# Four modulation vectors in two pairs on three engines, and weight folds moved by one chunk, in a diffusion block's mixer

## The chip, the cores and the metric

One core of one Trainium2 chip. The metric is the device time of one execution in microseconds (us), smaller is better. Times below are the median of several executions, and one profiled execution, whose trace is read here. TensorE multiplies matrices, VectorE and ScalarE and GpSimd work on tiles in SBUF (the on-chip memory, 128 partitions), SyncE only issues DMAs. Each engine works through its own queue of instructions in order; a DMA that is issued from ScalarE's queue stands in that queue too.

## The reference, cut to what matters

```python
sh1, sc1, g1, sh2, sc2, g2 = split(silu(c) @ w_ada + b_ada, 6)      # each 2048 long
h = rms_norm(x, norm1_g) * (1 + sc1) + sh1                           # 512 latent, 256 context rows
q, k, v, g, z_f, z_b, u = split(h @ w_in)                            # 2048 x 4128
o = bidirectional chunked gated linear attention(q, k, v, gates(z_f, z_b))
y = concat(norm(o) * gla_norm_g * silu(g), real part of a 2-D DFT of u)
x = x + g1 * (y @ w_out)
h2 = rms_norm(x, norm2_g) * (1 + sc2) + sh2
x = x + g2 * expert_choice_moe(h2)                                   # 16 experts, top 64 rows each
return rms_norm(x, final_norm_g)
```

Everything is float32. The first two vectors of the modulation (sh1, sc1) come early, in another form. The four "modulation vectors" of this document are numbers 2 to 5: g1, sh2, sc2 and g2. Each is a product of a 2048-long vector with a 2048 x 2048 matrix of 16.8 MB, read once.

## The kernel before, in words

Pages: `PG` holds 24 buffers of 128 x 2048 float32 (1 MB each), handed out first in, first out. A page that is given back may be taken at once; the new user's first instruction then waits until the last instruction of the old one is done. `PG.get()` with no page free makes the planner run a waiting background step early (`bg.force`).

Stages in order: the modulation's first part with the k columns (to about 150 us), the small z columns, the v columns (two groups c = 0, 1 of eight weight chunks each, six row tiles per chunk: four latent, two context), the q columns (eight chunks), the g columns (two groups of eight), the u columns (sixteen folded chunks), the output projection (four column groups c of eight chunks, the last four of each folded), the router, and the experts in eight pairs. Matmuls are done in three passes on a rounded high part and a low part.

Weights of the projections come through `Stream` (lines 166 to 215). A chunk (512 KB) is loaded by `load` from ScalarE's queue into one half of `rawp`. `split` takes a page, ScalarE copies the chunk into its first half rounded (line 203), VectorE writes the rest into its second half (line 204). `take(j)` splits up to chunk j + 1 before chunk j is used, `done(j)` gives the page back after TensorE's last matmul on it. Folded chunks (u columns, last four of each projection group) first go through `fold`: VectorE adds the halves (line 189), GpSimd subtracts them (line 190).

Background work is put between the matmuls by `Background`: after each row tile the foreground calls `bg.tick(us)`, in planner units (1.3 per tile in the v and q columns), and every generator that is due runs to its next `yield delay`. This fixes the order of instructions in each queue; the time at which they run is the chip's.

`ada_rest(i, delay)` (line 458) makes modulation vector i. It takes one page as accumulator; then for each of 16 steps it loads one page of `w_ada2` from the sync queue and adds page x scalar to the accumulator on VectorE (line 470 for the first, 472 for the others), and gives the page back. It keeps up to two pages loaded (`depth=2`): the one for this step and, if a page is free at that moment, the next one:

```python
for k in range(NK):
    while nl < min(k + depth, NK) and (nl == k or PG.free):
        ring[nl] = PG.get()
        sync.dma_start(ring[nl], a["w_ada2"][i - 2, nl])
        nl += 1
```

After the steps come four column sums on TensorE (line 478), a copy, transposes by matmul (line 483) and small additions. Before the change, `rest1` runs vectors 2, 4 and 3 one behind the other from the start of the v columns at 3.4 units per step; `rest2` drains it in the output projection, computes `logit_row`, and runs vector 5 at 4.6 units.

What holds pages in the v columns: HL (rounded latent rows, 8), HC (rounded context rows, 4, given back after v), rawp, W2, KT, KCM, VC (one each), V (one, then two), two rounded chunks, and the modulation's accumulator and ring.

In the projection, when a column group ends, four blocks of X (the residual state) are updated on VectorE (lines 1022 to 1026), and `logits` transposes them for the router. `pump` loads the experts' pages into whatever is free once `rest2` is done, from the third group on.

Of the kernel before, what the change touches and what calls it, by code (L numbers as in the profile page):

```python
# [17 lines left out]
AF = mybir.ActivationFunctionType  # L18
OP = mybir.AluOpType
# [11 lines left out]
C_F8, C_SCAN, C_MF, C_MB, C_FOLD, C_F, C_S8, C_ALL = 342, 350, 1118, 1246, 1374, 1470, 3297, 3881  # L31
F_CT, F_ST, F_ROW, F_CC, F_SC, F_K64, F_ALL = 0, 514, 1026, 1283, 1411, 1539, 1827
FW0 = 48
RD = (3.4, 4.6)
AD = (4.0, 2.5)
FD = (2.5, 1.8)
LD = (3.0, 7.0)
YD = (2.0, 3.0, 3.0, 5.0, 2.0, 1.0, 2.0, 2.0, 2.0)


# [62 lines left out]
def body(tc, nc, a, out, sb, pp):  # L103
    sync, act, dve, pe, pool = nc.sync, nc.scalar, nc.vector, nc.tensor, nc.gpsimd
    bg = Background()
# [5 lines left out]
    def tmp():  # L111
        tpi[0] = (tpi[0] + 1) % 4
        return TP[:, tpi[0], :]
# [14 lines left out]
    scol = sb.tile([128, NK], F32, name="scol")  # L128
# [17 lines left out]
    def v3(p, k):  # L146
        return p.rearrange("p (k n) -> p k n", k=k)


    X = [PG.get() for _ in range(4)]  # L150
# [15 lines left out]
    class Stream:  # L166
# [10 lines left out]

        def load(self, q=act):
            if self.nl < len(self.chunks) and self.nl < (max(self.ns, self.nf) if self.ns in self.folded else self.ns) + 2:
                q.dma_start(self.raw(self.nl), self.chunks[self.nl])  # L180
                self.nl += 1

        def fold(self, j):
# [9 lines left out]
        def split(self):  # L193
            n = self.ns
            self.load()
            self.fold(n)
            if self.ahead and n + 1 in self.folded:
                self.load()
                self.fold(n + 1)
                self.load()  # L200
            src = self.fw[n % 2] if n in self.folded else self.raw(n)
            p = PG.get()
            act.activation(p[:, :1024].bitcast(F32R), src, AF.Copy)  # L203
            dve.tensor_sub(p[:, 1024:].bitcast(F32R), src, p[:, :1024])  # L204
            self.parts[n] = p
            self.ns += 1

        def take(self, j):
            while self.ns < min(j + self.hd, len(self.chunks)):
                self.split()  # L210
            w = self.parts[j].rearrange("p (s k n) -> p s k n", s=2, k=2).bitcast(F32R)
            return w[:, 0], w[:, 1]

        def done(self, j):
# [3 lines left out]
    ws = Stream([a["w_in"][i] for i in range(W0)] + [a["w_out"][i] for i in range(32)],  # L218
                set(range(FW0, W0)) | {W0 + 8 * c + j for c in range(4) for j in range(4, 8)})
# [235 lines left out]
    bg.add(gate_rows(), 3.0)  # L455


    def ada_rest(i, delay, depth=2):

        acc = PG.get()  # L460
        ring = {}
        nl = 0
# [3 lines that stand above are left out]
                sync.dma_start(ring[nl], a["w_ada2"][i - 2, nl])  # L466
                nl += 1
            p = ring.pop(k)
            if k == 0:
                dve.tensor_scalar(acc, p, scol[:, 0:1], None, op0=OP.mult)  # L470
            else:
                dve.scalar_tensor_tensor(acc, p, scol[:, k:k + 1], acc, op0=OP.mult, op1=OP.add)  # L472
            PG.put(p)
            yield delay
        yield AD[0]
        b = BK.get()
        for j in range(4):
            pe.matmul(b[32 * j:32 * j + 32, :], ones[:, :32], acc[:, j * 512:(j + 1) * 512], start=True, stop=True)
        t = acc[:, :512]
        act.copy(t, b)  # L480
        yield AD[1]
        for q in range(4):
            pe.matmul(b[:, 4 * q:4 * q + 4], t[:, q * 128:(q + 1) * 128], sel4, start=True, stop=True)
        o, bias = {2: (gc[:, 0, :], bg1), 3: (b2, bsh2), 4: (a2, bsc2), 5: (gc[:, 1, :], bg2)}[i]

        def qj(x):
            return x.rearrange("p (j q) -> p q j", q=4)
        dve.tensor_add(qj(o), b[:, :NK].rearrange("p (q j) -> p q j", q=4), qj(bias))
        if i == 4:
            dve.scalar_tensor_tensor(a2, a2, 1.0, n2c, op0=OP.add, op1=OP.mult)  # L490
        BK.put(b)
        PG.put(acc)
# [11 lines left out]
            yield 1.3  # L504

    def rest(*vectors):
        for i, delay in vectors:
            yield from ada_rest(i, delay)

    rest1 = rest((2, RD[0]), (4, RD[0]), (3, RD[0]))  # L510
    bg.add(rest1)


    def tokens(j0, tiles, evac, last=False):
# [38 lines left out]
    for j in range(8):  # L553
        whi, wlo = ws.take(24 + j)
        for n in range(NH):
            for kk in range(2):
                k = 2 * j + kk
# [293 lines left out]
        BK.put(b)  # L851

    def rest_out():
        bg.drain(rest1)
        yield from logit_row()
        yield from rest((5, RD[1]))

    rest2 = rest_out()

# [50 lines left out]

    bg.drain(hfold)
    ws.ahead = True
    bs = [BK.get() for _ in range(4)]
    for k in range(NK):
        whi, wlo = ws.take(FW0 + k)
        for t, f in enumerate(lat):
            h = (f(k, 0), f(k, 1))
            i = t // 2
# [17 lines left out]
    X = [PG.get() for _ in range(4)]  # L936
# [39 lines left out]
    def logits(c, t):  # L976

        b = BK.get()
        for j in range(4):
            pe.transpose(b[:, j * 128:(j + 1) * 128], X[t][:, (4 * c + j) * 128:(4 * c + j + 1) * 128], ident)  # L980
        if not XT:
            XT.append(PG.get())
            lgb.append(BK.get())
        xtv = v3(XT[0], 4)
        act.copy(xtv[:, :, t * 128:(t + 1) * 128], v3(b, 4))
        BK.put(b)
        yield LD[1]
        for j in range(4):
            pe.matmul(lgb[0][32 * j:32 * j + 32, t * 128:(t + 1) * 128], awr[:, 4 * c + j, :],
                      xtv[:, j, t * 128:(t + 1) * 128], start=c == 0 and t == 0, stop=c == 3 and t == 3, skip_group_check=True)  # L990

    for c in range(4):
        bs = [BK.get() for _ in range(4)]
        cs = slice(c * 512, c * 512 + 512)
        order = [(j, t) for j in range(8) for t in range(4)]
        if c == 3:
            order = order[:16] + [(j, t) for t in (0, 2, 1, 3) for j in range(4, 8)]
        for n, (j, t) in enumerate(order):
            if (j, t) == (4, 0):
                bg.drain(gen)  # L1000
            whi, wlo = ws.take(W0 + 8 * c + j)
            i, ts = t // 2, slice(t * 128, (t + 1) * 128)
            for k, q in ((2 * j, 0), (2 * j + 1, 1)) if j < 4 else ((4 + j, i),):
                h = [yt(k, s)[:, ts] for s in range(2)]
                pe.matmul(bs[t], h[0], whi[:, q, :], start=k == 0, stop=False, skip_group_check=True)  # L1005
                pe.matmul(bs[t], h[0], wlo[:, q, :], start=False, stop=False, skip_group_check=True)  # L1006
                pe.matmul(bs[t], h[1], whi[:, q, :], start=False, stop=k == 11 and t == 3, skip_group_check=True)  # L1007
            if t == 2 and j >= 4:

                for s, w in ((0, whi), (0, wlo), (1, whi)):  # L1010
                    pe.matmul(bs[2][0:1, :], dT[:, j - 4, s:s + 1], w[:, 0, :], start=False, stop=False,
                              skip_group_check=True)
            if t < 3 and j == 7:

                y = Y64[0][0:72, ts if t < 2 else slice(256, 257)].bitcast(F32R)
                pe.matmul(bs[t][0:128 if t < 2 else 1, :], y, W64[0][0:72, cs].bitcast(F32R), start=False, stop=True,
                          skip_group_check=True)
            bg.tick(1.3 if j < 4 else 0.75)
            if j == 7 and t >= 2:
                t0 = t - 2  # L1020
                ps, qs = tmp(), tmp()
                dve.tensor_mul(ps, bs[t0], g1[0][:, cs])
                dve.tensor_mul(qs, bs[t], g1[0][:, cs])
                for x, f in ((X[t0][:, cs], dve.tensor_sub), (X[t][:, cs], dve.tensor_add)):
                    dve.tensor_add(x, x, ps)
                    f(x, x, qs)
                for r in (t0, t):
                    act.activation(ps if r == t0 else qs, X[r][:, cs], AF.Square, accum_out=ssx[:, r, c:c + 1])
                    bg.add(logits(c, r), LD[0])
            if t == 3:  # L1030
                ws.done(W0 + 8 * c + j)
            if c == 3 and (j, t) == (3, 3):
                PG.put(*YG[0], *YG[1])
            if (c, j, t) == (2, 7, 3):
                bg.drain(rest2)
            if c >= 2 and t == 3 and not bg.has(rest2):
                ws.hd = 4
                pump(keep=max(0, min(ws.hd - len(ws.parts), len(ws.chunks) - ws.ns)))
        BK.put(*bs)
# [161 lines left out]
    for pr in range(8):  # L1201
        gu = [BK.get() for _ in range(4)]
        for kg in range(8):
# [9 lines left out]
            ps = [wp.pop(wi + i) for i in range(4)]  # L1213
            wi += 4
            for m in range(2):
                if pr == 0 and m and kg < 7:
                    gather(0, 2 * kg + 2, 2)
                for k2 in range(2):
                    k = 2 * kg + k2
# [45 lines left out]
        for c in range(4):  # L1265
# [7 lines left out]
            for f in range(2):  # L1273
                if f and c and not last:
                    combine(pr, c - 1)
                ps = [wp.pop(wi + i) for i in range(2)]
# [33 lines left out]
    for c in range(4):  # L1310
        acc = v3(ACC[c], 4)
        cs = slice(c * 512, c * 512 + 512)
        for t in range(4):
            if c >= 2:
                dve.scalar_tensor_tensor(acc[:, t, :], acc[:, t, :], rsf[:, t:t + 1], FG[0][:, cs], op0=OP.mult,
                                         op1=OP.mult)
# [113 lines left out]
```

## Time and profile before

| | us |
|---|---|
| median of 3 runs | 1890.49 (1885.64 to 1891.79) |
| profiled execution | 1892.82 |
| its span | 1891.0 |
| TensorE busy | 1702.4 (90%) |
| VectorE busy | 761.1 (40%) |
| ScalarE busy | 343.3 (18%) |
| GpSimd busy | 82.9 (4%) |

A trace's times count from the span's start. PE is TensorE's matmuls, PEld its weight loads, DVE VectorE, ACT ScalarE, POOL GpSimd, SP SyncE; a name with q behind it is that engine's queue. `L472` is line 472 of the kernel. In groups, "idle before" is the time for which an engine stood just before such an instruction, with what ended it. `pg<-in_w_ada` is a load into a page from the modulation weights.

### The profile page before, as it was taken

The page shows a single profiled execution, that of the slowest core. Times are in us where ns is not written, and L with a number is a line of the kernel's source. Part 1 is how long each engine was busy: PE and PEld are TensorE (multiplying, and loading weights), DVE is VectorE, ACT ScalarE, POOL GpSimd, SP SyncE. Part 2 cuts the span into 40 slices and gives each one's busy share as a digit, 9 for nine tenths or more (in the row PEclk, how much of TensorE's full clock was granted, in tenths as well). Part 3 has the DMA queues.
Part 4 walks back from the last instruction along what each step waited for, and adds up shares of the span by engine and source line. Part 5 has one row for each costly group of instructions (what it writes and reads, how often), then busy time and mean ns, then how long its engine had stood idle before and what let it go on. Part 6 is the DMA issues. An engine that isn't in the chain of part 4 may idle for free.

```text
span 1891.0 us, 21143 instructions
## 1 busy us (share of the span) xinstructions
PE 1702.4 (90%) x8756; PEld 1011.0 (53%) x8756; DVE 761.1 (40%) x1188; ACT 343.3 (18%) x593; POOL 82.9 (4%) x61
## 2 busy tenths in 40 slices
PE   5999999897677798888999999999999999999885
PEld 4777887686455586665455444444444444444322
DVE  5335677837656647654323113131120311303005
ACT  4222111335443412222000000000000000000013
POOL 0000000001222101111000000000000000000000
PEclk9999999998888899998999999999999999999998
DMA  9955788621124336626796999999999999999996
GB/s 380 382 216 205 296 307 316 243 67 56 34 69 157 133 134 218 237 96 280 320 363 252 391 419 419 420 419 420 420 419 420 420 419 420 420 419 417 407 420 260
DMA packets 89760, 572.36 MB, mean 303 GB/s; under 512 B 9872, under 2 KB 12344, under 8 KB 27176
## 3 DMA queue, kind: packets, MB, share of 16 engines
q1 hardware_dynamic: 75720, 521.44, 68.3%
q10 hardware_dynamic: 13944, 49.56, 7.6%
q8 instruction: 69, 1.13, 0.2%
q14 instruction: 27, 0.22, 0.0%
HBM read 566.77 MB, written 4.19 MB: 302 GB/s over the span
## 4 chain that ended last, share of the span: by engine, by line
PE 38%; DMA 18%; DVE 6%; ACT 2%; issue 1%; POOL 0%; ACTq 0%; DVEq 0%; SPq 0%; POOLq 0%
PE bank L1222 16%; DMA pg<-in_w_e_up 10%; PE bank L1281 9%; PE bank L1141 5%; DMA pg<-in_w_e_down 4%; PE bank L1184 2%; DMA pg<-in_w_e_gate 2%; DMA pg<-in_w_out 2%; DVE pg L204 1%; ACT pg L203 1%; PE bank L1006 1%; PE bank L1007 1%; PE bank L1005 1%; DVE pg L472 1%; PE bank L501 0%
## 5 line engine op out<-in xcount | busy, mean ns | idle before, releaser
L1222 PE MATMUL bank<-pg,pg 128*64 128x512 f32 x1856 | 435.2, 597 | 25.8 <-DMA pg<-in_w_e_up 14.2
L1222 PEld LDWEIGHTS bank<-pg,pg 128*64 128x64 f32 x1856 | 139.2, 136 | 287.8 <-issue 218.1
L1281 PE MATMUL bank<-pg,tp 128*64 128x512 f32 (+1 forms) x1056 | 233.3, 584 | 11.7 <-ACT tp L1249 10.8
L204 DVE TENSOR_TENSOR pg<-pg,pg 128x1024 fp32r<-128x1024 f32 x96 | 122.5, 1280 | 109.5 <-ACT pg L203 95.2
L1145 DVE TENSOR_SCALAR pg<-bank,a,b 128x128 f32<-128x128 f32 x116 | 41.4, 405 | 302.6 <-PE bank L1141 302.6
L1281 PEld LDWEIGHTS bank<-pg,tp 128*64 128x64 f32 x1056 | 74.5, 137 | 145.8 <-issue 124.1
L472 DVE SCALAR_TENSOR_TENSOR pg<-pg,scol,pg 128x2048 f32<-128x2048 f32 x60 | 140.9, 2349 | 27.1 <-DMA pg<-in_w_ada 26.6
L203 ACT ACTIVATE pg<-pg 128x1024 fp32r<-128x1024 f32 x96 | 100.9, 1058 | 268.7 <-DVE pg L472 79.3
L523 PE MATMUL bank<-pg,pg 128*128 128x512 f32 x320 | 131.8, 412 | 13.6 <-ACT pg L203 13.6
L1187 DVE TENSOR_TENSOR pg<-pg,bank 128x512 f32<-128x512 f32 (+1 forms) x132 | 79.6, 666 | 152.9 <-PE bank L1184 152.9
L524 PE MATMUL bank<-pg,pg 128*128 128x512 f32 x320 | 128.8, 402 | 2.2 <-DVE pg L204 2.2
L525 PE MATMUL bank<-pg,pg 128*128 128x512 f32 x320 | 128.1, 400 | 0.0
L1141 PEld LDWEIGHTS bank<-pg,pg 128*128 128x128 f32 x896 | 104.0, 192 | 32.1 <-issue 29.2
L1141 PE MATMUL bank<-pg,pg 128*128 128x128 f32 x896 | 111.5, 279 | 0.0
L1256 ACT ACTIVATE tp<-bank 128x512 f32<-128x512 f32 x16 | 9.4, 597 | 431.4 <-PE bank L1222 431.4
L1005 PE MATMUL bank<-pg,pg 128*128 128x512 f32 x192 | 80.3, 418 | 5.5 <-ACT pg L203 5.5
L1006 PE MATMUL bank<-pg,pg 128*128 128x512 f32 x192 | 78.5, 409 | 5.7 <-DVE pg L204 5.7
L523 PEld LDWEIGHTS bank<-pg,pg 128*128 128x128 f32 x320 | 62.3, 195 | 30.4 <-ACT pg L203 14.9
L1007 PE MATMUL bank<-pg,pg 128*128 128x512 f32 x192 | 77.1, 402 | 0.0
L1285 DVE SCALAR_TENSOR_TENSOR pg<-bank,gcol,pg 128x512 f32<-128x512 f32 (+1 forms) x33 | 24.2, 735 | 125.1 <-PE bank L1281 125.0
L360 PE MATMUL bank<-pg,pg 128*128 128x512 f32 x192 | 71.8, 374 | 0.9 <-ACT pg L350 0.8
L524 PEld LDWEIGHTS bank<-pg,pg 128*128 128x128 f32 x320 | 62.4, 195 | 15.8 <-DVE pg L204 3.3
(318 smaller groups left out, 1974.2 us busy)
## 6 DMA issues: line engine op xcount, KB each, us to landing
pg<-in_w_e_gate SPq DMA_DIRECT2D x128, 1024.0 KB, 19.9
pg<-in_w_e_up SPq DMA_DIRECT2D x128, 1024.0 KB, 8.0
pg<-in_w_e_down SPq DMA_DIRECT2D x126, 1024.0 KB, 19.9
pg<-in_w_ada SPq DMA_DIRECT2D x96, 1024.0 KB, 7.6
pg<-in_w_in ACTq DMA_DIRECT2D x62, 512.0 KB, 4.4
pg<-in_w_out ACTq DMA_DIRECT2D x32, 512.0 KB, 3.4
pg<-in_x SPq DMA_DIRECT2D x4, 1024.0 KB
pg<-in_x_slots SPq DMA_DIRECT2D x4, 1024.0 KB, 12.4
```

The costliest lines, as they stand in the source:

```text
L203: act.activation(p[:, :1024].bitcast(F32R), src, AF.Copy)
L204: dve.tensor_sub(p[:, 1024:].bitcast(F32R), src, p[:, :1024])
L472: dve.scalar_tensor_tensor(acc, p, scol[:, k:k + 1], acc, op0=OP.mult, op1=OP.add)
L523: pe.matmul(bs[t], h[0], whi[:, kk, :], start=k == 0, stop=False)
L524: pe.matmul(bs[t], h[0], wlo[:, kk, :], start=False, stop=False)
L525: pe.matmul(bs[t], h[1], whi[:, kk, :], start=False, stop=k == 15)
L1005: pe.matmul(bs[t], h[0], whi[:, q, :], start=k == 0, stop=False, skip_group_check=True)
L1006: pe.matmul(bs[t], h[0], wlo[:, q, :], start=False, stop=False, skip_group_check=True)
L1007: pe.matmul(bs[t], h[1], whi[:, q, :], start=False, stop=k == 11 and t == 3, skip_group_check=True)
L1141: pe.matmul(b[:, j * 128:(j + 1) * 128], X[t][:, k * 128:(k + 1) * 128], ohr[:, t, :], start=t == 0, stop=t == 3)
L1222: pe.matmul(gu[2 * m + f][64 * j:64 * j + 64, :], xe(pr, k)[:, 64 * j:64 * j + 64], v3(ps[2 * m + j], 2)[:, k2, f * 512:f * 512 + 512], st ...
L1281: pe.matmul(b[64 * j:64 * j + 64, :h.stop - h.start], hidt[:, 4 * f + k, 64 * j:64 * j + 64], v3(ps[j], 4)[:, k, h], start=f == 0 and k == ...
```

## The change

Vectors 2 and 4 stay on VectorE; vectors 3 and 5 form a second generator that runs beside the first from the v columns on, with ScalarE scaling each loaded page in place and GpSimd adding it to the accumulator. Both run at 5.0 units per step. Vector 5 leaves the output projection. `split` now folds the next chunk after it has rounded this one (before: ahead of rounding), and the first fold is done ahead of the u columns. Folded chunks load from the sync queue. Two of four updates of X per pair of row tiles go to GpSimd, and two delays of `logits` are longer.

```diff
-RD = (3.4, 4.6)
+RD = (5.0, 5.0)
-LD = (3.0, 7.0)
+LD = (5.0, 7.0)
 ...
-                q.dma_start(self.raw(self.nl), self.chunks[self.nl])
+                (sync if self.nl in self.folded else q).dma_start(self.raw(self.nl), self.chunks[self.nl])
 ...
             self.load()
             self.fold(n)
-            if self.ahead and n + 1 in self.folded:
-                self.load()
-                self.fold(n + 1)
-                self.load()
             src = self.fw[n % 2] if n in self.folded else self.raw(n)
             p = PG.get()
             act.activation(p[:, :1024].bitcast(F32R), src, AF.Copy)
             dve.tensor_sub(p[:, 1024:].bitcast(F32R), src, p[:, :1024])
             self.parts[n] = p
             self.ns += 1
+            if self.ahead or (self.fw and self.ns == FW0):
+                self.load()
+                self.fold(self.ns)
+                self.load()
 ...
-    def ada_rest(i, delay, depth=2):
+    def ada_rest(i, delay, e=dve, depth=2):
 ...
-            if k == 0:
-                dve.tensor_scalar(acc, p, scol[:, 0:1], None, op0=OP.mult)
+            if e is pool:
+                act.activation(p if k else acc, p, AF.Copy, scale=scol[:, k:k + 1])
+                if k:
+                    pool.tensor_add(acc, acc, p)
+            elif k == 0:
+                e.tensor_scalar(acc, p, scol[:, 0:1], None, op0=OP.mult)
             else:
-                dve.scalar_tensor_tensor(acc, p, scol[:, k:k + 1], acc, op0=OP.mult, op1=OP.add)
+                e.scalar_tensor_tensor(acc, p, scol[:, k:k + 1], acc, op0=OP.mult, op1=OP.add)
 ...
-    rest1 = rest((2, RD[0]), (4, RD[0]), (3, RD[0]))
+    rest1 = rest((2, RD[0]), (4, RD[0]))
+    restp = rest((3, RD[1], pool), (5, RD[1], pool))
     bg.add(rest1)
+    bg.add(restp, 2.0)
 ...
     def rest_out():
-        bg.drain(rest1)
+        bg.drain(restp)
         yield from logit_row()
-        yield from rest((5, RD[1]))
 ...
     ws.ahead = True
+    ws.load()
+    ws.fold(ws.ns)
 ...
-                for x, f in ((X[t0][:, cs], dve.tensor_sub), (X[t][:, cs], dve.tensor_add)):
-                    dve.tensor_add(x, x, ps)
+                for x, e, f in ((X[t][:, cs], pool, pool.tensor_add), (X[t0][:, cs], dve, dve.tensor_sub)):
+                    e.tensor_add(x, x, ps)
                     f(x, x, qs)
 ...
-                    bg.add(logits(c, r), LD[0])
+                    bg.add(logits(c, r), LD[0] if r == t0 else LD[0] + 2.0)
```

## Rows read from the trace of the kernel before

**Rows 1.** By stage: length; PE, PEld, DVE, ACT, POOL busy; clock; DMA; GB/s.

```profile
162.00:308.00 146.00, 141.09 (x616) 113.42 (x614) 99.25 (x64) 25.52 (x30) 0.00 (x0) 0.96 0.78 288
308.00:352.00 44.00, 44.00 (x196) 36.43 (x195) 37.08 (x23) 10.37 (x12) 0.00 (x0) 1.00 1.00 408
...
526.00:657.00 131.00, 100.31 (x457) 73.58 (x456) 79.33 (x139) 51.40 (x89) 25.74 (x18) 0.87 0.35 122
657.00:882.00 225.00, 198.95 (x971) 150.07 (x969) 130.17 (x134) 57.31 (x88) 31.76 (x16) 0.95 0.49 177
...
912.00:1870.00 958.00, 918.24 (x4570) 411.27 (x4570) 205.18 (x444) 57.91 (x106) 0.00 (x0) 1.00 0.97 399
```

**Rows 2.** PE's waits for rounding, 162 to 352 us: total, times, longest.

```profile
PE bank L523 <- ACT pg L203: 2.0, 1, 2.0
PE bank L524 <- DVE pg L204: 0.8, 1, 0.8
```

**Rows 3.** Waits of SyncE (162 to 355 us) and of L203: total, times.

```profile
SPq L466 <- DVE pg L472: 56.9, 21, 4.4
SPq L466 <- PE bank L525: 22.7, 7, 8.8
...
  DVE pg L472: 79.3, 10
```

**Rows 4.** Timeline of DVE in c = 1: start, duration [idle before].

```profile
248.27 2.35 DVE L472 SCALAR_TENSOR_TENSOR pg<-pg,scol,pg 128x2048 f32<-128x2048 f32 x1 [1.25 <-DMA pg<-in_w_ada]
250.88 2.35 DVE L472 SCALAR_TENSOR_TENSOR pg<-pg,scol,pg 128x2048 f32<-128x2048 f32 x1 [0.25 <-DMA pg<-in_w_ada]
255.50 2.35 DVE L472 SCALAR_TENSOR_TENSOR pg<-pg,scol,pg 128x2048 f32<-128x2048 f32 x1 [2.27 <-DMA pg<-in_w_ada]
```

**Rows 5.** The 64 modulation loads of line 466, from issue to landing.

```profile
DMA to landing us min/median/max: 4.8/7.0/11.6
```

**Rows 6.** Groups by line: busy us, mean ns of one, idle before.

```profile
L472 DVE SCALAR_TENSOR_TENSOR pg<-pg,scol,pg 128x2048 f32<-128x2048 f32 x60 | 140.9, 2349 | 27.1 <-DMA pg<-in_w_ada 26.6
L204 DVE TENSOR_TENSOR pg<-pg,pg 128x1024 fp32r<-128x1024 f32 x96 | 122.5, 1280 | 109.5 <-ACT pg L203 95.2
L203 ACT ACTIVATE pg<-pg 128x1024 fp32r<-128x1024 f32 x96 | 100.9, 1058 | 268.7 <-DVE pg L472 79.3
L263 ACT ACTIVATE pg<-pg 128x2048 f32<-128x2048 f32 x6 | 11.4, 1899 | 1.2 <-DMA pg<-in_x 1.2
L478 PE MATMUL bank<-pg,cst 128*32 128x512 f32 x32 | 4.3, 605 | 0.0
L882 POOL TENSOR_TENSOR pg<-pg,pg 128x512 f32<-128x512 f32 x16 | 20.5, 1280 | 94.1 <-DVE pg L885 81.8 <-ACT pg L883 12.3
L641 POOL MEMSET pg<- 128x1024 f32 x4 | 3.8, 948 | 247.0 <-DVE pg L472 247.0
L162 POOL MEMSET spad<- 128x512 f32 x1 | 0.5, 524 | 0.3 <-POOLq L1418 0.3
```

**Rows 7.** The two halves of a fold: ns of one, min/median/max.

```profile
L190 POOL TENSOR_TENSOR pg<-pg x32: 1261/1721/3333, 504.6 to 860.3; 128x512 f32<-128x512 f32 x32
L189 DVE TENSOR_TENSOR pg<-pg x32: 667/691/1782, 515.4 to 860.2; 128x512 f32<-128x512 f32 x32
```

**Rows 8.** Timeline of PE in the v columns, two matmuls left out between.

```profile
214.56 0.39 PE L523 MATMUL bank<-pg,pg 128*128 128x512 f32 x1
...
215.24 0.39 PE L523 MATMUL bank<-pg,pg 128*128 128x512 f32 x1
```

**Rows 9.** PE's waits for rounding, 526 to 882 us.

```profile
PE bank L919 <- ACT pg L203: 12.7, 7, 2.7
...
PE bank L920 <- DVE pg L204: 5.8, 7, 0.8
PE bank L1006 <- DVE pg L204: 5.7, 9, 0.8
PE bank L1005 <- ACT pg L203: 5.5, 3, 2.0
```

More of the change, by code (lines that the diff above doesn't have):

```diff
@@ L506, in rest @@
     def rest(*vectors):
-        for i, delay in vectors:
-            yield from ada_rest(i, delay)
-    rest1 = rest((2, RD[0]), (4, RD[0]), (3, RD[0]))
+        for v in vectors:
+            yield from ada_rest(*v)
+    rest1 = rest((2, RD[0]), (4, RD[0]))
+    restp = rest((3, RD[1], pool), (5, RD[1], pool))
     bg.add(rest1)
+    bg.add(restp, 2.0)
     def tokens(j0, tiles, evac, last=False):
```

## The prediction

> **What bounds the kernel now.** I read the stages first, then who waits for whom in each stage, then the order of instructions in the stage that the change fills, and last the durations from which new work can be priced. In the experts the DMA engines are taken to 0.97 at 399 GB/s [rows 1]: that stage is bound by its weights and only moves as a block when the mixer ends earlier or later. So the change is worth what it does to the time before 912 us. There, TensorE sets the pace of the v and q columns: it is busy for 141 of 146 us and 44 of 44 [rows 1], and waits for rounded weights for 2.8 us in all [rows 2]. In the u columns and the output projection it idles 131 - 100 = 31 and 225 - 199 = 26 us, at a granted clock of 0.87 and 0.95 [rows 1].
>
> What the busy shares don't show is the pages. `PG` has 24. During the v columns HL holds 8, HC 4, and rawp, KT, KCM, W2, VC and V one each: 18, and 19 in the second column group (c = 1). The rounded weights hold 2 at a time. That leaves 4 pages, then 3, for a modulation vector: one accumulator and a ring of two just fit. The trace shows how tight that is: the sync queue stood 56.9 us waiting for a VectorE product to give back a page and 22.7 us for TensorE to finish a chunk, and the copy that rounds weights waited 79.3 us for such products [rows 3]. With two pages the loads are just hidden: the product at 255.50 us reads the page that the one at 248.27 gave back at 250.62, so 4.9 us from release to use, which includes the 2.27 us for which VectorE stood [rows 4].
>
> **The change part by part.** The profiled execution took 1892.82 us (span 1891.0, the rest outside it), 2.3 above the median of the three runs; I add to 1892.8.
>
> *Two vectors at once.* Vectors 2 and 4 stay on VectorE, 3 and 5 go to ScalarE (a scaling copy) and GpSimd (an add), each with a step every 5.0 planner units. The q columns' end lies 96 x 1.3 + 32 x 1.3 = 166.4 units in, 190 us, so a pair of steps, one of each vector, is meant to take 5.7 us. But there are now two accumulators. In c = 0 the two rings share 4 - 2 = 2 pages, in c = 1 they share 3 - 2 = 1. `ada_rest` only loads ahead while `PG.free` is not empty; the list is empty after nearly every load, so each load is put down at its own step, into the page that the step before has just given back. A load then starts when that step ends, and lands, at the shortest, 4.8 us after issue [rows 5]; a second one issued with it lands 1.049 MB / 408 GB/s = 2.6 us later (that rate: [rows 1], where DMA is at 1.00), so at 7.4.
>
> Prices: product on VectorE 2.35; scaling copy 1.90 (the 128x2048 activation); rounding 1.06 on ScalarE and 1.28 on VectorE [rows 6]. No row has a 128x2048 add on GpSimd. Four of 128x512 are 4 x 1.28 = 5.1 [rows 6], and 4 x 1.72 = 6.9 at the median of those that run beside VectorE's own half of a fold [rows 7]. Below: a memset of twice the columns costs 0.948 against 0.524, so 0.10 is fixed, and one large add saves 0.3: 4.8 [rows 6]. I take 5.1, since in the chain below VectorE mostly stands while GpSimd adds. The Trainium skill (GPSIMD Engine Reference, 3.1 Elementwise) gives 4.497 us for this very add; by that alone the sum below would be about 18 us shorter (30 adds x 0.6). No row here shows it.
>
> c = 0, the chain of pages. Two chunks are 12 x 1.3 = 15.6 units, so three pairs fall in them. Twice the end of a GpSimd add frees a page, the sync queue (in order) issues VectorE's load and then GpSimd's, and the latter's page goes on: 7.4 + 1.9 + 5.1 = 14.4 each. The third time the page goes to the next rounded chunk: 1.06 + 1.28 for the rounding, behind which VectorE's product stands in its queue (2.35), and only its page lets the next load go: 4.8 + 1.9 + 5.1. That is 16.5. Sum 45.3 per three pairs, 15.1 per pair, against 5.7 planned. Matmuls start 0.227 us apart [rows 8], so a chunk's 36 take 8.2 and TensorE needs 16.4 of those 45.3: it waits. Sixteen pairs, to the end of vectors 2 and 3: 16 x 15.1 = 242.
>
> Change of vectors: column sums on TensorE 8 x 0.134 = 1.1 (4.3 us for 32, [rows 6]) and a copy of about 0.6, then a first load and product, and behind it, on the same page, a load and a copy: 4.8 + 2.35 + 4.8 + 1.9. Together 16: 258.
>
> c = 1: one page for both. Strictly in turn a pair costs 4.8 + 2.35 + 4.8 + 1.9 + 5.1 = 18.9; where a finished chunk lends a second page, 14.4. I take the middle, 16.7. The last v chunk can be rounded when pair 4 of the second vectors has given its page back: 258 + 4 x 16.7 = 325, + 2.3 + 8.2 = 335 for the end of v (146 before).
>
> q: HC's four pages come free, the ring is four pages again and loads go in twos, two pairs per 14.4. Pairs 5 to 7 were already queued on the one page: 325 + 50 = 375; pairs 8 to 13 at 7.2, 418; the last chunk's rounding and matmuls 2.3 + 5.5: **426 us for v and q, where 190 were: +236**. Bounds: adds at 4.8, -9; at 6.9, +50; landing at its median of 7.0 [rows 5], which holds loads queued behind others, in half the steps, +37; all of c = 1 at 14.4 a pair, -18.
>
> Each new wait stands in an in-order queue: ScalarE's scaling copy ahead of the rounding copy and of the weight loads issued from that queue, VectorE's product ahead of the rounding subtraction, GpSimd's add with nothing behind it, the column sums ahead of all matmuls. The rounding waits besides for the page itself.
>
> *What is taken away later.* The rest of vector 3 and all of vector 5 (its sixteen products at 2.35 are 37 us of VectorE) leave the g columns and the output projection; folds go behind the rounding of the chunk before, so that its subtraction no longer stands behind a fold that waits for its load; folded chunks load from the sync queue, past ScalarE's work. TensorE's waits for rounding between 526 and 882 us are 12.7 + 5.8 + 5.7 + 5.5 = 29.7 [rows 9]: this is all that these edits can return directly. The clock lay at its lower level for 2 x 0.13 x 131 + 2 x 0.05 x 225 = 57 us there, in which at most half was lost, 28. Bounds 0 and -58; I take **-25**, most of the direct waits, since what is late next (logits' copies, folds' loads) stays.
>
> *Small edits.* Two of eight state updates per column group go from VectorE to GpSimd: two adds at 1.28 beside two at 0.69, no later than the four in a row that they replace; zero. LD's delays fill with the same matmuls; zero. Expert loads may start earlier in the projection, but pages, not time, limit them before 912; zero. A folded load in the sync queue can stand behind an expert page: up to 2.6 us for some of the last four folded chunks, +10 at most, within the bounds.
>
> Sum: 1892.8 + 236 - 25 = **2104**. Ends: 1892.8 + 236 - 9 - 18 - 58 = 2044 and 1892.8 + 236 + 50 + 37 + 0 = 2216.
>
> **The rivals.**
> 1. *Pages don't bind and the change does what it says (faster).* Loads run ahead, only the transfer rate is left: 64 pages and 24 chunks of w_in are 67.1 + 12.6 = 79.7 MB, at 408 GB/s 195 us, 5 more than now: 1892.8 + 5 - 25 = 1873, at best 1840. For it: VectorE would be emptier. Against it: SyncE's and ScalarE's waits for pages with one vector [rows 3]. It decides at four free ring pages beside the 21 held and two accumulators: 27 of 24. Chance 0.05.
> 2. *The rings share pages but overlap better.* If each page's round (15 to 19) overlapped fully with the other's, c = 0 would go at about 8 a pair and only c = 1 would starve: 16 x 8 + 16 + 67 + 10 = 221 for v, 312 for v and q: +122, 1990. Against: in-order queues tie the rounds together. Chance 0.06.
> 3. *GpSimd and VectorE hold each other up.* A fold's half on VectorE took up to 1.782 us where 0.667 is the least, on GpSimd up to 3.333 against 1.261 [rows 7]. If every add stretched to 4 x 3.33 = 13.3, the 24 pairs of v alone would cost 24 x 8.2 = 197 more: 2300. The Trainium skill (GPSIMD Engine Reference, 1. Specifications) says that GpSimd's SBUF interfaces are shared with VectorE, with contention from instructions with two SBUF inputs; those rows agree. Against it: VectorE stands idle for most of each round. Chance 0.04.
>
> **How the numbers follow.** Forecast 0.85, rivals 0.05, 0.06, 0.04. Case 1 alone is faster by over 0.3% (5.7 us, about what a measurement can tell from no change); 0.02 for the band around zero, where gain and loss happen to meet; the rest, 0.93, slower. The range is the forecast's own, 2044 to 2216, a little wider below for a partial overlap: 2030 to 2216.
>
> **What would show it.** The v and q columns reach from 162 to about 590 us instead of 352, with TensorE's busy share near 0.45, waiting for the rounding copy, and that copy waiting for GpSimd's add and VectorE's product. Modulation loads issue one at a time just after such steps end, with DMA near 79.7 MB / 426 us = 187 GB/s, and the adds take about 5.1 us. From g columns on everything lies later by the same amount, less some 25 us by the end of the projection; the experts' stage keeps its 958 us. Wrong would be: loads issued a step or more ahead of use in c = 0, or TensorE's share above 0.8 there.

## The result and the profile after

The changed kernel takes **2103.18 us** (median of three, 2099.54 to 2103.97) against 1890.49: a ratio of 1.113, interval 1.109 to 1.116. The prediction was 2104. The profiled execution is the median one, with a span of 2101.2. Stages, cut where TensorE's matmuls of a stage begin and end:

| stage | before, us | after, us | difference |
|---|---|---|---|
| v and q columns | 190 | 440 | +250 |
| g columns | 174 | 169 | -5 |
| u columns | 131 | 119 | -12 |
| projection | 222 | 198 | -24 |
| to the first expert matmul | 36 | 39 | +3 |

Together with a start 3 us earlier this is the 209 us by which the first expert matmul moved (915.5 to 1124.0). The experts moved as a block. Line numbers below are those of the changed kernel where no other run is named: 199 is the rounding copy (203 before), 200 the rounding subtraction, 470 ScalarE's scaling copy, 472 GpSimd's add, 476 VectorE's product (472 before), 482 the column sums, 487 the transposes behind them, 529 and 360 the first matmuls on a chunk in the v and the q columns. The stages of after, in the columns of [rows 1], the first line being v and the second q:

```profile
159.00:503.00 344.00, 182.85 (x623) 135.70 (x621) 87.04 (x50) 66.36 (x49) 85.83 (x19) 0.72 0.41 155
503.00:600.00 97.00, 55.41 (x193) 40.62 (x193) 60.60 (x21) 30.16 (x23) 49.43 (x10) 0.79 0.66 263
...
768.00:887.00 119.00, 96.24 (x456) 71.30 (x457) 76.65 (x139) 51.44 (x89) 27.20 (x18) 0.91 0.33 116
887.00:1086.00 199.00, 189.71 (x934) 145.49 (x932) 87.58 (x100) 55.64 (x86) 44.75 (x31) 0.97 0.35 121
1120.00:2078.00 958.00, 918.43 (x4554) 410.87 (x4556) 205.52 (x446) 57.84 (x105) 0.00 (x0) 1.00 0.97 399
```

No engine is the bound of the v columns: TensorE is busy for 183 of 344 us, VectorE for 87, ScalarE for 66, GpSimd for 86, and DMA has a share of 0.41. A stage in which everything is half idle is one in which things happen in turn. Who waits shows what turns: TensorE for the rounding copy, 163 us in 18 waits where [rows 2] had one of 2.0:

```profile
PE bank L529 <- ACT pg L199: 128.5, 13, 23.1
PE bank L360 <- ACT pg L199: 34.9, 5, 14.2
```

ScalarE for loads ahead of its scaling copy (line 470), and the rounding copy (line 199) for pages that products and adds still hold:

```profile
ACT pg L470 <- DMA pg<-in_w_ada: 244.2, 27, 17.0
ACT pg L199 <- DVE pg L476: 53.7, 8, 12.0
ACT pg L199 <- POOL pg L472: 37.2, 8, 4.7
```

And the loads, in SyncE's queue, for pages, 304 us where [rows 3] had 57 for products:

```profile
SPq L466 <- POOL pg L472: 200.8, 18, 17.9
SPq L466 <- DVE pg L476: 103.4, 12, 13.9
```

So the circle is closed: load waits for page, copy for load, add for copy, page for add, and the rounding stands in the same queues. Its period is seen on GpSimd, in the timeline of after:

```profile
199.23 4.51 POOL L472 TENSOR_TENSOR pg<-pg,pg 128x2048 f32<-128x2048 f32 x1 [11.74 <-ACT pg L470]
213.36 4.54 POOL L472 TENSOR_TENSOR pg<-pg,pg 128x2048 f32<-128x2048 f32 x1 [9.62 <-ACT pg L470]
227.51 4.49 POOL L472 TENSOR_TENSOR pg<-pg,pg 128x2048 f32<-128x2048 f32 x1 [9.61 <-ACT pg L470]
243.71 4.51 POOL L472 TENSOR_TENSOR pg<-pg,pg 128x2048 f32<-128x2048 f32 x1 [11.71 <-ACT pg L470]
```

From start to start these are 14.1, 14.2 and 16.2 us, the three kinds of round that were worked out as 14.4, 14.4 and 16.5; three pairs take 44.5 us.

Of the signs that the prediction named, TensorE's share of v and q came out at 0.54 and not 0.45. The granted clock was 0.72 and 0.79 there, so the same matmuls kept TensorE busy for 183 + 55 = 238 us where they took 185 before; since TensorE waits for the rounding copy anyway, the pages still set the time.

### The profile page after: what moved, and what is told of

Read it like the earlier page. It is cut to its first block, busy times and chain, and to the rows that moved or that the text cites. A ratio compares the mean times of both kernels' runs of the same rounds, so it can differ in the third digit from the quotient of the medians.

```text
span 2101.2 us, 21219 instructions
## 1 busy us (share of the span) xinstructions
PE 1742.4 (83%) x8756; PEld 1030.0 (49%) x8756; DVE 727.5 (35%) x1140; ACT 405.9 (19%) x625; POOL 240.8 (11%) x107
## 4 chain that ended last, share of the span: by engine, by line
PE 43%; DMA 11%; DVE 3%; ACT 1%; issue 0%; ACTq 0%; DVEq 0%; SPq 0%
PE bank L1229 16%; PE bank L1288 10%; DMA pg<-in_w_e_up 7%; PE bank L1148 6%; DMA pg<-in_w_e_gate 3%; PE bank L1191 3%; PE bank L1012 2%; PE bank L1013 2%; PE bank L1014 2%; DMA pg<-in_w_e_down 1%; DVE pg L1033 1%; PE bank L1018 1%; PE bank L505 0%; ACT tp L1256 0%; DVE pg L200 0%
## 5 line engine op out<-in xcount | busy, mean ns | idle before, releaser
L1229 PE MATMUL bank<-pg,pg 128*64 128x512 f32 x1856 | 435.0, 597 | 26.0 <-DMA pg<-in_w_e_up 14.1
L529 PE MATMUL bank<-pg,pg 128*128 128x512 f32 x320 | 145.5, 455 | 134.7 <-ACT pg L199 132.0
L200 DVE TENSOR_TENSOR pg<-pg,pg 128x1024 fp32r<-128x1024 f32 x96 | 150.3, 1567 | 292.8 <-ACT pg L199 284.3
L472 POOL TENSOR_TENSOR pg<-pg,pg 128x2048 f32<-128x2048 f32 x30 | 142.0, 4733 | 346.1 <-ACT pg L470 345.9
L530 PE MATMUL bank<-pg,pg 128*128 128x512 f32 x320 | 141.9, 443 | 24.6 <-DVE pg L200 24.6
L529 PEld LDWEIGHTS bank<-pg,pg 128*128 128x128 f32 x320 | 69.1, 216 | 161.5 <-ACT pg L199 138.2
L531 PE MATMUL bank<-pg,pg 128*128 128x512 f32 x320 | 138.0, 431 | 0.0
L476 DVE SCALAR_TENSOR_TENSOR pg<-pg,scol,pg 128x2048 f32<-128x2048 f32 x30 | 87.8, 2926 | 93.8 <-DMA pg<-in_w_ada 93.7
L1148 PEld LDWEIGHTS bank<-pg,pg 128*128 128x128 f32 x896 | 103.9, 192 | 32.1 <-issue 28.4
L470 ACT ACTIVATE pg<-pg,scol 128x2048 f32<-128x2048 f32 x32 | 64.1, 2004 | 244.2 <-DMA pg<-in_w_ada 244.2
L360 PE MATMUL bank<-pg,pg 128*128 128x512 f32 x192 | 75.5, 393 | 35.7 <-ACT pg L199 34.9
L530 PEld LDWEIGHTS bank<-pg,pg 128*128 128x128 f32 x320 | 69.4, 217 | 45.3 <-DVE pg L200 31.1
L1012 PE MATMUL bank<-pg,pg 128*128 128x512 f32 x192 | 79.6, 415 | 3.4 <-ACT pg L199 3.4
L1013 PE MATMUL bank<-pg,pg 128*128 128x512 f32 x192 | 76.7, 400 | 1.4 <-DVE pg L200 1.4
```

What stands on the lines that cost most here:

```text
L472: pool.tensor_add(acc, acc, p)
L529: pe.matmul(bs[t], h[0], whi[:, kk, :], start=k == 0, stop=False)
L530: pe.matmul(bs[t], h[0], wlo[:, kk, :], start=False, stop=False)
L531: pe.matmul(bs[t], h[1], whi[:, kk, :], start=False, stop=k == 15)
L1148: pe.matmul(b[:, j * 128:(j + 1) * 128], X[t][:, k * 128:(k + 1) * 128], ohr[:, t, :], start=t == 0, stop=t == 3)
L1229: pe.matmul(gu[2 * m + f][64 * j:64 * j + 64, :], xe(pr, k)[:, 64 * j:64 * j + 64], v3(ps[2 * m + j], 2)[:, k2, f * 512:f * 512 + 512], st ...
```

## The experiments

The first theory was the prediction's: pages. Its rivals were that GpSimd and VectorE hold each other up, and sheer load.

**Four more pages.** Edit of the changed kernel:

```diff
-    ctxt = [lambda k, s, t=t: hc(k, s)[:, t * 128:(t + 1) * 128] for t in range(2)]
+    ctxt = [lambda k, s, t=t: hl(k, s)[:, t * 128:(t + 1) * 128] for t in range(2)]
+    for i in range(2):
+        PG.put(*HC.pop(i))
 ... (and no longer after the v columns)
```

> The changed kernel with four more free pages: the context tiles of the v columns read latent rows, so that HC's four pages are given back before the v columns and not after them. That part of the computation is other data, the matmuls, copies and their number are the same; engines, delays and order rules too. Theory (pages): 27 pages are wanted in c = 1, 28 are now there, loads run a step ahead; v and q take what 79.7 MB need at 408 GB/s, 195 to 205 us, where the changed kernel took 440; time 2103 - 240 = 1863, range 1845 to 1880. Rival (GpSimd and VectorE hold each other up, or ScalarE's scaling copy delays the rounding): pages change little, v and q stay above 330 us, time above 1990.

1916.78 us (1912.08 to 1923.34), ratio to before 1.013 (1.010 to 1.017): 186 us of the 213 lost came back by pages alone, since engines, delays and the count of everything stayed; v and q fell from 440 to 251. That settles the main cause. But the forecast was 1863, and v and q were to take 195 to 205 us. The windows of v and q (columns as above) and VectorE's timeline of this run show a different bound:

```profile
161.00:413.00 252.00, 207.43 (x815) 161.11 (x813) 220.22 (x70) 93.84 (x69) 162.76 (x29) 0.88 0.79 310
```

```profile
182.32 5.63 DVE L200 TENSOR_TENSOR pg<-pg,pg 128x1024 fp32r<-128x1024 f32 x1
187.88 13.32 DVE L476 SCALAR_TENSOR_TENSOR pg<-pg,scol,pg 128x2048 f32<-128x2048 f32 x2
201.12 1.21 DVE L200 TENSOR_TENSOR pg<-pg,pg 128x1024 fp32r<-128x1024 f32 x1
202.26 6.69 DVE L476 SCALAR_TENSOR_TENSOR pg<-pg,scol,pg 128x2048 f32<-128x2048 f32 x1
```

VectorE is now busy for 220 of 252 us, with the same instructions that were 1.2 and 2.35 us long: some last 5.6 and 6.7. So a second cause stands behind the first.

**Two more pages**, the same edit for half of the channels (`hl if k >= 8 else hc`, `HC.pop(1)` ahead of v).

> As the run with four more pages, but only two: the context tiles of the v columns read latent rows for the second half of the 2048 channels only (that part is other data), and two of HC's four pages are given back before the v columns. Theory (pages): in c = 0 two rings of two fit, in c = 1 three ring pages serve two vectors; a VectorE round of a page is 4.8 + 2.35 = 7.2, a ScalarE and GpSimd round 4.8 + 2.0 + 4.5 = 11.3, together 18.5 page-us per pair or 6.2 per pair with three pages where 5.7 is planned: v and q 200 to 240 us, time 1860 to 1905. Rival: not pages, time above 1990.

1934.19 us (1923.13 to 1935.91), ratio 1.021 (1.018 to 1.025), v and q 265: only 17 us above four pages, 169 below none. Two pages are nearly enough. The forecast of 1860 to 1905 missed. The second cause is at work here too (products last up to 6.7 us, GpSimd's adds 5.2 at the median), and pages still bind in part: the rounding copy waits 39.6 us for pages that adds hold. How the 25 us beyond the forecast's 240 for v and q divide between the two stays open.

**Both streams on VectorE, pages as in the change.**

```diff
-    restp = rest((3, RD[1], pool), (5, RD[1], pool))
+    restp = rest((3, RD[1]), (5, RD[1]))
```

> The changed kernel with vectors 3 and 5 on VectorE too, so that nothing of the modulation is on ScalarE or GpSimd; the two generators, their delays, and the pages stay. Theory (pages): the round of a page gets shorter by the copy and the add, not free: in c = 0 three pairs take 7.4 + 2.35, again 9.75, then 1.06 + 1.28 + 2.35 + 4.8 + 2.35, together 31.3 or 10.4 a pair; 16 pairs 167, change of vectors 14, four pairs in c = 1 at 12, rounding and chunk 10, q 67: v and q about 307 us where 440 were, time near 1970 (1920 to 2020). Rival (GpSimd and VectorE hold each other up): with GpSimd out of it v and q fall to 200 to 220, time near 1870. Rival (sheer load on VectorE or DMA): no better than 2100.

2002.47 us (2001.41 to 2005.86), ratio 1.059 (1.056 to 1.061), v and q 336 where the chain gave 307. The time is within the range and far from both rivals: with neither ScalarE nor GpSimd in the modulation the starved rings still cost 112 us over before. Why v and q took 29 us more than the chain stays open. The rounding copy now waits almost only for products, and TensorE mostly for the copy; the copy's waits from 159 to 400 us and TensorE's from 159 to 420:

```profile
ACT pg L199 <- DVE pg L476: 196.1, 11, 37.8
```

```profile
PE bank L529 <- ACT pg L199: 67.6, 10, 16.7
```

**Four pages and both streams on VectorE**, the two edits together. This takes GpSimd's adds out of a kernel that has its pages.

> The changed kernel with HC's four pages given back before the v columns (the context tiles of the v columns read latent rows: that part is other data, the same count of everything) and with vectors 3 and 5 on VectorE too, so without GpSimd's adds. With the four pages alone v and q took 251 us, not 195 to 205: GpSimd's adds and VectorE's instructions on two SBUF inputs seemed to take turns (30 x 4.5 + 30 x 2.35 + 24 x 1.23 = 236). Theory (they take turns): without the adds VectorE has 62 x 2.35 + 24 x 1.23 = 175 us of work in v and q, the loads 195: v and q 195 to 210, time 1858 to 1880. Rival (the four pages still don't suffice, or the transfer rate holds it): as with the four pages alone, v and q near 250, time 1905 to 1925.

1860.01 us (1856.69 to 1864.83), ratio 0.983 (0.980 to 0.986), v and q 195. All four vectors then fit into v and q, at the transfer rate, with DMA at 0.98:

```profile
161.00:357.00 196.00, 185.13 (x814) 148.76 (x813) 170.96 (x101) 35.72 (x42) 0.00 (x0) 0.97 0.98 394
```

The 57 us between this and the run with four pages are the price of moving half of the products off VectorE. This edit takes away ScalarE's scaling copies too, so the next two runs measure GpSimd's part by itself.

**Adds and memsets that nobody needs, in the kernel before.**

```diff
+    def extra():
+        scr = TP.rearrange("p a n -> p (a n)")
+        pool.memset(scr, 0.0)
+        for _ in range(30):
+            pool.tensor_add(scr, scr, scr)      # or twice pool.memset(scr, 0.0)
+            yield 5.0
+    bg.add(extra(), 8.0)
```

> The kernel before with 30 more GpSimd adds of 128x2048 on the scratch tile (two SBUF inputs, result unused), one each 5.0 units in the v and q columns; nothing else depends on them. Theory (GpSimd's and VectorE's instructions on two SBUF inputs take turns): VectorE is busy for 136 us of v and q, the adds take 30 x 4.5 = 135; in turn they are 271, so v and q go from 190 to 240 to 275, time 1940 to 1975. Rival (separate engines, no mutual wait): v and q 190 to 195, time 1888 to 1896.

> As the run with 30 more GpSimd adds, but each add is two memsets of the same 128x2048 tile (about 2 x 1.8 = 3.6 us, no SBUF input). Theory (it is reads that the two engines share): no mutual wait, v and q 190 to 195, time 1888 to 1896, memsets at 1.8 to 1.9 each. Rival (any GpSimd access to SBUF holds VectorE): v and q 220 to 260, time 1920 to 1960.

Adds: 1963.26 us (two executions, 1958.53 and 1967.98), ratio 1.038 (1.034 to 1.041), v and q 261. Memsets: 1891.26, ratio 1.000 (0.999 to 1.002), v and q 191. Nothing waits for either by a semaphore, so what the adds cost is taken from VectorE while it runs. GpSimd's group and VectorE's product (min/median/max; line 472 as in the kernel before) in the run with adds:

```profile
L517 POOL TENSOR_TENSOR tp<-tp 128x2048 f32<-128x2048 f32 x30 | 154.0, 5134 | 2.4
```

```profile
L472 DVE SCALAR_TENSOR_TENSOR pg<-pg,scol,pg x60: 2325/2352/5686, 165.8 to 860.0; 128x2048 f32<-128x2048 f32 x60
```

and with memsets:

```profile
L518 POOL MEMSET tp<- 128x2048 f32 x60 | 109.8, 1830 | 3.5
```

```profile
L472 DVE SCALAR_TENSOR_TENSOR pg<-pg,scol,pg x60: 2325/2350/2354, 165.7 to 792.2; 128x2048 f32<-128x2048 f32 x60
```

While GpSimd adds, a product lasts up to 5.7 us; while it only writes, never over 2.354. What the adds do and the memsets don't is to read SBUF, so reading is the likely point of contact; no run takes the adds' reading apart from the rest of what they do. In this run the two don't take full turns: an add and a product one behind the other would be 4.53 + 2.35 = 6.9 us, near the 6.7 seen with four pages, and here a pair took about 5.6. Nor did the memsets leave everything alone. A vector's first step, with one page as input and 1.28 us long elsewhere, ran beside them and lasted 2.25:

```profile
232.07 2.25 DVE L470 TENSOR_SCALAR pg<-pg,scol 128x2048 f32<-128x2048 f32 x1
```

**Before with four more pages**, a control.

> The kernel before with HC's four pages given back before the v columns (the context tiles of the v columns read latent rows: that part is other data, the same count of everything). A control for the two runs on pages. Theory: with one vector at a time three pages suffice and the loads are just hidden, so 1886 to 1893, no change; v and q 190. Rival (pages held the kernel before as well): v and q shorter by up to the 2.8 us of waits and time below 1885.

1881.17 us (1879.84 to 1886.3), ratio 0.995 (0.993 to 0.997), v and q 184. The theory was wrong by a little: even with one vector the pages cost the kernel before some 9 us, 6 of them in v and q. There TensorE's 2.8 us of waits for rounding were gone, and the granted clock was 0.99 over both, where v had 0.96 and q 1.00 [rows 1]. "Just fit" was not quite true, and the runs with four pages hold that much of gain which has nothing to do with the change.

**The later parts alone**: the changed kernel with `RD = (3.4, 4.6)`, vectors 2, 4, 3 in `rest1`, and 5 in `rest_out`, as before.

> The changed kernel with the vectors as before (2, 4 and 3 on VectorE one behind the other at 3.4 units, 5 in the projection at 4.6): only the folds behind the rounding, folded loads in the sync queue, two updates of X on GpSimd and logits' delays are left of the change. In the changed kernel the g columns took 168 us (before 173), the u columns 119 (131), the projection 203 (225), together -39. Theory: the folds' part is the u columns' -12 and about half of the projection's -22, the other half is vector 5's removal: time 1890 - 23 = 1867, range 1855 to 1880. Rival (all of the later gain is vector 5's removal): 1885 to 1892. Rival (all of it is the folds): 1852 to 1856.

1871.35 us (1869.41 to 1873.14), ratio 0.989 (0.987 to 0.992). u 120, projection 213: the folds, their queue and the small edits are worth 11 and 9 us there, within the theory's range, and the projection's remaining 13 to 15 (198 to 200 in every run without vector 5 in it) go with vector 5.

**Without the updates on GpSimd**: that kernel, all of X's updates on VectorE, `LD = (3.0, 7.0)`.

> The run that keeps only the later parts of the change (1871 us), with all updates of X back on VectorE and logits' delays as before, so that only the folds behind the rounding and the folded loads in the sync queue are left. It computes everything. Theory (the updates on GpSimd are worth nothing, the folds all): 1868 to 1875, projection 211 to 216. Rival (the updates on GpSimd shorten the end of each column group, or hold VectorE up): 5 us or more away, projection above 218 or below 208.

1866.4 us (1863.94 to 1868.76), ratio 0.987 (0.985 to 0.990); projection 211. The time lies just below the theory's 1868 to 1875, 5 us under the run with the updates. The intervals of the two ratios overlap, so whether those updates cost anything isn't settled; that they bring something isn't seen. This is the fastest of the kernels that compute everything, 1.3% below the kernel before.

**Vector 5 begun in the u columns.**

```diff
     def rest_out():
-        yield from rest((5, RD[1]))
+        bg.drain(rest5)
 ...
+    rest5 = rest((5, RD[1]))
 ... (at the head of the u columns)
+    bg.add(rest5, 12.0)
```

> The run that keeps only the later parts of the change (1871 us), with vector 5 still on VectorE at 4.6 units but begun 12 units into the u columns and not behind the router's row in the projection, where its pages and VectorE have room. It computes everything. Theory (vector 5 is what holds the projection at 213 us against 198 to 200 without it): the projection falls to 200 to 206, the u columns grow by 0 to 8, time 1858 to 1870. Rival (its cost only moves along with it): u and projection together stay at 333, time 1868 to 1876.

1900.0 us (1894.07 to 1900.99), ratio 1.005 (1.003 to 1.007): both expectations missed. u took 137 and the projection 222. The edit did not take vector 5 out of the projection. Seven of its sixteen products were still to come when the projection began; they were drained end to end, from 667 to 684 us, and the column sums stood in TensorE's queue behind them. TensorE's waits from 520 to 860 us in this run show it, with more waiting for rounding in u:

```profile
PE bank L482 <- DVE pg L476: 16.9, 1, 16.9
PE bank L927 <- ACT pg L199: 16.8, 5, 6.0
```

The wait for column sums alone is longer than the 9 us by which the projection grew over the later parts alone. Against it, TensorE's transposes of X, which waited 9.7 + 0.9 = 10.6 us for VectorE's updates of X in that run, waited 2.5 in this one. In u the waits for rounding grew by 7.7 us, and the granted clock was 0.84 against 0.91; how its 17 us divide stays open. So the theory, that vector 5 holds the projection, was tested only in part.

## Why the prediction was right

**Pages, the main term.** Right in mechanism, shown by giving pages back. Step by step, from the start of the v columns: the last add of the sixteenth pair ends after 240.5 us, predicted 242; the first steps of the second vectors are done at 261, predicted 258; pair 4 at 331 against 325 (a pair in c = 1 took 17.4, taken as 16.7); end of v at 343 against 335; q 97 against 91. Sum 440 against 426.

The unknown price, the add, was taken as 5.1. Where VectorE mostly stands it lasts 4.53, the source view of after:

```profile
L472 POOL TENSOR_TENSOR pg<-pg,pg x30: 4492/4531/5952, 182.9 to 601.4; 128x2048 f32<-128x2048 f32 x30
```

That is the value of the Trainium skill (GPSIMD Engine Reference, 3.1 Elementwise), 4.497, to 1%, and below my lower bound of 4.8; my estimate by it was a sum about 18 us shorter. Modulation loads landed in 4.8 at the median, as taken, the source view of line 466:

```profile
DMA to landing us min/median/max: 4.7/4.8/9.0
```

That 242 came out so near is in part luck, since errors met. The round of three pairs was 44.5 and not 45.3: three shorter adds gave back 1.7, and scaling copies of 2.01 instead of 1.90, with some tenths between steps, took about half of that. And eight chunks of c = 0 hold, at three pairs for two chunks, only twelve of the sixteen pairs; the last four ran with the pages of c = 1 and took 62.9 us, 15.7 each, where the first twelve took 14.8.

The rounding's subtraction, 1.22 us alone, met an add in each of these rounds and lasted 4.76. This cost the chain nothing in c = 0:

```profile
200.06 4.76 DVE L200 TENSOR_TENSOR pg<-pg,pg 128x1024 fp32r<-128x1024 f32 x1 [5.58 <-ACT pg L199]
208.53 2.35 DVE L476 SCALAR_TENSOR_TENSOR pg<-pg,scol,pg 128x2048 f32<-128x2048 f32 x1 [3.71 <-DMA pg<-in_w_ada]
```

The add beside it ran from 199.23 to 203.74, and the next two loads were issued at 203.76. The subtraction ended 1.08 us after the add, and VectorE then stood for 3.71 us until its load had landed. Only TensorE waited for the subtraction, 4.3 us, ahead of a wait of 17.6 for the next chunk.

The change of vectors took 20.7 us, not 16, the step that was sized worst in v. Vector 4's first load wanted a page that came free with vector 2's transposes, and these stood in TensorE's queue behind a chunk whose rounding waited for vector 3's last add; SyncE's waits from 159 to 600 us:

```profile
SPq L466 <- PE bank L487: 24.4, 2, 17.6
```

In q, adds that run beside products last up to 5.95 us, and two pairs take 16.4, not 14.4.

**The third rival** had the right mechanism and the wrong place. I gave it 0.04 because VectorE stands idle for most of each round, and in the starved kernel that holds. It is the next bound behind the pages: with four pages v and q came to 251, near the 30 x 4.53 + 30 x 2.35 + 24 x 1.22 = 236 of taking turns. The first rival, that the change does what it says, assumed 1873 where pages suffice; with four more pages it was 1917. The second, 8 us a pair by overlap, is ruled out by the 14.8 of c = 0. The Trainium skill names the sharing (GPSIMD Engine Reference, 1. Specifications) and the extra adds agree with it.

**The later gain** was mis-sized: -25 taken, about -38 measured to the first expert matmul, 36 of it in the u columns and the projection. The step at fault is "all that these edits can return directly". Waits for rounding fell from the 29.7 of [rows 9] to 8.4 + 4.4 + 3.4 + 1.4 = 17.6, so they returned 12. TensorE's other waits in these two stages fell as well, from 26.1 to 14.5, and the prediction had left them out. Most of that is the transposes of X in `logits` (line 980 before, 987 after), which wait for X's updates on VectorE (1022, 1026) and for the copies of earlier transposes (985); before, from 526 to 882 us:

```profile
PE bank L980 <- ACT pg L985: 5.9, 3, 2.5
PE bank L980 <- DVE tp L1022: 2.8, 2, 2.0
PE bank L980 <- DVE pg L1026: 2.5, 1, 2.5
```

After, from 768 to 1086 us:

```profile
PE bank L987 <- DVE pg L1033: 1.7, 2, 0.9
PE bank L987 <- PE bank L987: 0.8, 1, 0.8
```

With the later parts alone they were still 10.6, so their shortening goes with vector 5's absence and not with the small edits. The rest is the clock: granted 0.87, then 0.91 in u and 0.95, then 0.97 in the projection, it lay at its lower level for 57 us before and 33 after, worth at most 12; the three parts can hold the 36. By the runs, folds and queue hold about 20 to 24 of the total and vector 5 13 to 15.

**Small edits** at zero: the updates of X measured 0 to 5 us against, not settled. Expert loads brought nothing, as taken: the experts' stage is 958 us in both.

The errors, +14 in v and q, -13 later and -3 at the start, cancelled in the total; that 2104 met 2103 so closely is luck.

## What to carry to other kernels

Before work is put beside other work, count the buffers that it holds at the fullest moment, not only engine time: here two accumulators and two rings wanted 27 of 24 pages, and the fallback (load at the step itself) turned a pipeline into a chain without any engine, queue or transfer looking busy. When engines and DMA are all half idle in a stage, follow one buffer round and add up its stops. And an add moved from VectorE to GpSimd was not free for VectorE here: thirty adds that nothing waited for made the kernel before 3.8% slower.

## What the runs showed of the hardware

GpSimd's 128x2048 float32 add takes 4.53 us where VectorE mostly stands, and 5.13 on average among the thirty extra adds beside a busy VectorE. VectorE's instructions on two SBUF inputs that meet such adds last 4.6 to 6.7 us instead of 1.22 to 2.35, about one per add. Sixty memsets on GpSimd, 1.83 us each, left products at 2.35 and the total unchanged; one tensor_scalar with one page as input lasted 2.25 us beside them instead of 1.28.
